# All gates of a hybrid S5 / mLSTM block by a seven-product block scheme, in two phases

## The chip, the cores and the metric

The kernel runs on one core of one Trainium2 chip. The metric is the device time of one execution in microseconds (us). The core has a tensor engine (PE, with its weight loads shown as PEld), VectorE (DVE), ScalarE (ACT), GpSimd (POOL) and SyncE (SP). SP issues nearly all transfers, POOL a few; all data that doesn't fit on chip passes through DRAM.

## The reference

One decoder block for 1024 tokens, with 16 learned meta tokens ahead (LEN = 1040), and D_MODEL = 1024. What matters here:

```python
p = h @ w_in + b_in          # columns [u_s5 | q | k | v | o | i | f | g_s5 | g_m]
y_s5 = GLU(GELU(S5(u_s5)))   # z[:, :1024] * sigmoid(z[:, 1024:]), z = gelu(..) @ w_glu
hm   = HeadNorm(mLSTM(silu(conv(q, k)), v, i, f))          # 4 heads of 256
y_m  = (sigmoid(o) * hm) @ m_w_out
mix  = sigmoid(g_s5) * y_s5 + sigmoid(g_m) * y_m
h    = LN(alpha * h + mix @ w_o)
h    = LN(alpha * h + relu(h @ w_up + b_up)**2 @ w_down)
```

o, g_s5 and g_m are the three gates: each is a projection of h with 1024 columns, that is eight tiles of 128 features, followed by a sigmoid. All of it is float32.

## The kernel before

*Products.* Every float32 operand is split into a high part, rounded to the fast matmul format, and the remainder: hi on ScalarE (a copy), lo = x - hi on VectorE. A product is then three matmuls, hi*hi, hi*lo and lo*hi (`mm3`, L229; the matmuls themselves are L240 to L242). The normalised input, transposed, lies on chip as `hT_hi` and `hT_lo`.

*Jobs.* The first half of the kernel is a list of jobs in the order of the string `ORDER`: q (with k), v, u, o, g (g_s5), then eight GLU jobs, the g_m jobs and eight jobs of the output projection of the mLSTM (`ym_job`). A job has one or two weight tiles of 128 x 1024. They are fetched one or two jobs ahead by SP and split (`split_w`: whi L220, wlo L221) while the job before runs (`job.after`). The functions of o and g_s5 jobs are `o_job` and `gs_job`: 128 features, eight blocks of 128 inputs, two halves of 512 tokens, three matmuls each, so 48 matmuls. An o job multiplies its sigmoid onto the finished head, `HM`, at once (L921), so the main loop forces the mLSTM lane forward until the head is there (`HMREADY`).

*Lanes.* Beside the jobs there are generators for the work off PE's main stream: the convolution, the mLSTM (`mlstm`), S5 (`s5_batch`, four batches), the token sums (`t_prep`), the scaled residual (`ah_scale`) and an early part of the feed-forward weights (`up_early`). `pump` moves them forward as matmuls are issued, at paces given in `PACE`. A planner with a model of the engines then puts every instruction into its engine's queue. The queue of each engine is static and executed in order.

*Seven products.* The g_m gates are computed in pairs of feature tiles. The product of a 2 x 2 block matrix of weights (two feature tiles by two halves of the inputs) with a 2 x 2 block matrix of h (two halves of the inputs by two halves of the tokens) is made of seven block products rather than eight, with sums of weight blocks (`wsums`: n1, n2, on VectorE) and sums of token blocks (made once by `t_prep`, kept in `t_dr`). A block product is four blocks of 128 inputs by three matmuls, 12. Four pairs: the plain products come in two jobs (`gme_job`), the others in one long job (`gm_pairs`), which loads the sums over the room of `hT` (`t_hi`, `t_lo`, by POOL's queue). The feed-forward layers use the same scheme.

*After the jobs* come the projection w_o, a LayerNorm, and the two feed-forward layers, from about 800 us to the end. The change doesn't touch them.

Of the kernel before, what the change touches and what calls it, by code (L numbers as in the profile page):

```python
# [120 lines left out]
def decoder_block(  # L121
# [73 lines left out]
    class Job:  # L195
        def __init__(self, loads, run):
            self.loads, self.run = loads, run
            self.raw, self.w, self.tag, self.ran = None, None, None, set()

# [15 lines left out]
    def split_now(job, later=False):  # L215
        job.w = []
# [39 lines left out]
    e_dr = dram.tile([2, P, 512], F32, name="e_dr")  # L256
    sgm_dr = dram.tile([KT, P, SEQ], F32, name="sgm_dr")
# [52 lines left out]
    QK, VT, HM, HMREADY = {}, {}, {}, set()  # L310
# [152 lines left out]
    def mlstm(h):  # L463
# [67 lines left out]
        def N(half, hm):  # L531
# [7 lines left out]
            for f in range(2):  # L539
                if half == 0:  # L540
                    HM[2 * h + f] = slot("hmF")
                ps = sdps("pt")
                for i in range(4):
                    t_.transpose(ps[:, i * P:(i + 1) * P], hraw[:, i * DV + f * P:i * DV + (f + 1) * P], ident)
                a_.activation(HM[2 * h + f][:, half * 512:(half + 1) * 512], ps, AF.Copy,
                              scale=mngt[:, 2 * h + f:2 * h + f + 1])
                yield 1.2
# [13 lines left out]
        HMREADY.update((2 * h, 2 * h + 1))  # L561
# [352 lines left out]
    hm_dr = dram.tile([KT, P, D], F32, name="hm_dr")  # L914

    def o_job(f):
        def evac(bi, c0, c1, ps):
            if bi == 0:
                o_job.s = slot("osig")
            a_.activation(o_job.s[:, c0:c1], ps, AF.Sigmoid, bias=bft[:, JO + f:JO + f + 1])  # L920
            v_.tensor_tensor(HM[f][:, c0:c1], HM[f][:, c0:c1], o_job.s[:, c0:c1], op=OP.mult)  # L921

        def done():
            nc.sync.dma_start(hm_dr[f], HM.pop(f)[:, :D])
        fm_job(JO + f, HALF, META, evac, done)
# [19 lines left out]
    def gs_job(f):  # L945
        def evac(bi, c0, c1, ps):
            if bi == 0:
                SG[f] = slot("sgs")
            a_.activation(SG[f][:, c0:c1], ps, AF.Sigmoid, bias=bft[:, JGS + f:JGS + f + 1])
        fm_job(JGS + f, HALF, META, evac)  # L950

    def glu_job(f):
        def run(job):
            if f == 0:
                lanes["s5c"].drain()
                lanes["s5"].drain()
                lanes["s5g"].drain()
            (wh, wl), = job.w
# [61 lines left out]
    GT, GR, GW, GC, GE = {}, {}, {}, {}, {}  # L1020

    def gt_load(n, tiles):
        GT[n] = tiles
        for i in range(4):
            g_.dma_start(tiles[i], t_dr[n - 1, :, i // 2, 2 * (i % 2):2 * (i % 2) + 2, :].rearrange("p k s -> p (k s)"))

    def gme_job(*ps):
        def run(job):
            if ps[0] == 2:
                for p in range(4):  # L1030
                    gr_load(p)
                gt_load(2, [slot("gt", F32R)[:, 0:1024] for _ in range(4)])
            chain, e = {}, {}
            for q in range(2):
                for i, p in enumerate(ps):
                    wh, wl = job.w[i]
                    if q == 0:
                        chain[p] = mmps()
                        e[p] = slot("gme")
                    terms = [(wh[:, (4 * q + j) * P:(4 * q + j + 1) * P], wl[:, (4 * q + j) * P:(4 * q + j + 1) * P],  # L1040
                              bh, bl) for j, (bh, bl) in enumerate(hT_blk(q, 0))]
                    mm3(chain[p], terms, part=(q == 0, True), skip=q == 1)
                    if q == 0:
                        a_.activation(e[p][:, 0:512], chain[p], AF.Copy)
                        if i == 0:
                            job.after()
                    else:
                        a_.activation(e[p][:, 512:1024], chain[p], AF.Sigmoid, bias=bft[:, JGM + 2 * p:JGM + 2 * p + 1])
                        nc.sync.dma_start(sgm_dr[2 * p, :, 0:512], e[p][:, 512:1024])
                        if p < 2:  # L1050
                            nc.sync.dma_start(e_dr[p], e[p][:, 0:512])
                        else:
                            GE[p] = e[p]
                if ps[0] == 2:
                    for z in (2 * q, 2 * q + 1):
                        gr_sums(z)
                        gw_split(z, 3)
        all_jobs.append(Job([(wf[JGM + 2 * p].rearrange("p k f -> p (k f)"), 1024) for p in ps], run))

    def gr_load(p):  # L1060
        GR[p] = [slot("gmr"), slot("gmr")]
        for i in range(2):
            nc.sync.dma_start(GR[p][i][:, :D], wf[JGM + 2 * p + i].rearrange("p k f -> p (k f)"))
        if p < 2:
            GE[p] = slot("gme")
            nc.sync.dma_start(GE[p][:, 0:512], e_dr[p])

    def gr_sums(p):
        r0, r1 = GR[p]
        n1, n2 = wsums(r0[:, 0:512], r0[:, 512:1024], r1[:, 0:512], r1[:, 512:1024])  # L1070
        GR[p] = {3: n2[:, 0:512], 4: r1[:, 512:1024], 5: n1[:, 0:512], 6: n1[:, 512:1024], 7: r1[:, 0:512]}

    def gw_split(p, n):
        x = GR[p].pop(n)
        o = slot("gmw", F32R)
        a_.activation(o[:, 0:512], x, AF.Copy)
        v_.tensor_tensor(o[:, 512:1024], x, f32(o[:, 0:512]), op=OP.subtract)
        GW[p, n] = o
        if n == 4:
            GR.pop(p)  # L1080

    GSEQ = [(p, n) for n in (3, 6, 5, 7, 4) for p in range(4)]

    def g_step(p, n):
        w = GW.pop((p, n))
        e = GE[p]
        b1, b2 = (bft[:, JGM + 2 * p + i:JGM + 2 * p + i + 1] for i in range(2))
        if n in (3, 6):
            ps = mmps()
        elif n == 5:  # L1090
            ps = sdps()
        else:
            ps = GC[p, "b"]
        if n == 3:
            blk = hT_blk(1, 1)
        else:
            t = GT[{4: 4, 5: 1, 6: 2, 7: 3}[n]]
            blk = [(t[j // 2][:, (j % 2) * 512:(j % 2) * 512 + 512], t[2 + j // 2][:, (j % 2) * 512:(j % 2) * 512 + 512])
                   for j in range(4)]
        terms = [(w[:, j * P:(j + 1) * P], w[:, 512 + j * P:512 + (j + 1) * P], bh, bl)  # L1100
                 for j, (bh, bl) in enumerate(blk)]
# [906 lines left out]
```

## Time and profile before

| | |
|---|---|
| three runs | 1540.72, 1542.88 (median), 1544.22 us |
| profiled execution | span of 1538.6 us; the page gives no other time of it |
| sigmoids of the o and g_s5 jobs | 197 to 562 us |
| evacuation of the GLU jobs | 571 to 652 us |
| later products of the g_m pairs | 662 to 720 us |
| evacuation of the mLSTM's output projection | 725 to 814 us |
| ScalarE, POOL | 41% and 7% busy |

Busy time of PE is modelled, and a matmul's own duration (375 ns on average for 512 columns) overlaps with the next one's; their spacing is what counts. A busy share is an average over stages. A line such as L240 is that of a helper, so that rows are told apart by the tiles they write and read. Idle time of an engine that is not the bottleneck costs nothing.

### The profile page before, as it was taken

What the parts mean: (1) busy time and instruction counts of PE and PEld (TensorE: products, weight loads), DVE (VectorE), ACT (ScalarE), POOL (GpSimd) and SP (SyncE); (2) the same over time, 40 slices, a digit from 0 to 9 for tenths busy, and PEclk for the clock granted to TensorE, in tenths of its full rate; (3) what the DMA queues carried; (4) which work ended last, traced back from release to release, by engine and by line L of the source; (5) the groups of instructions that cost most, each with busy time, mean ns of one, the idle gap of its engine ahead of it and who ended that gap; (6) DMA issues with size and microseconds to landing.
All of it is one profiled execution on the core that took longest, in us unless ns stands there. A gap on an engine that the chain in (4) does not pass through costs nothing.

```text
span 1538.6 us, 20771 instructions
## 1 busy us (share of the span) xinstructions
PE 1514.8 (98%) x7652; PEld 1279.8 (83%) x7652; DVE 1061.5 (69%) x2062; ACT 625.8 (41%) x996; POOL 102.4 (7%) x180
## 2 busy tenths in 40 slices
PE   9999999999999999999999999999999999999997
PEld 9999978998888888878878887888888888888886
DVE  7567867668968758675348574766666689766786
ACT  6623455324264443234015243444444534433440
POOL 0000000432214000010000001000000000000000
PEclk9999999999999999999999999999999999999999
DMA  9402265522332689878243238544444897766642
GB/s 333 143 5 88 72 203 159 174 64 61 113 91 71 184 292 355 317 281 322 102 149 139 83 119 271 178 149 145 150 142 133 276 381 280 246 234 232 211 178 96
DMA packets 148597, 277.71 MB, mean 181 GB/s; under 512 B 18488, under 2 KB 69120, under 8 KB 148496
## 3 DMA queue, kind: packets, MB, share of 16 engines
q1 hardware_dynamic: 143168, 256.99, 49.7%
q0 software_dynamic: 5328, 19.40, 3.9%
q8 instruction: 60, 0.98, 0.3%
q14 instruction: 41, 0.34, 0.1%
HBM read 188.00 MB, written 87.17 MB: 179 GB/s over the span
## 4 chain that ended last, share of the span: by engine, by line
PE 64%; issue 27%; DVE 5%; DMA 2%; ACT 1%; POOL 0%; POOLq 0%; SPq 0%; DVEq 0%; ACTq 0%
PE mm L240 16%; PE mm L241 15%; PE mm L242 15%; PE sd L240 3%; PE sd L241 3%; PE sd L242 3%; PE mm L236 2%; PE mm L274 1%; PE pn L504 1%; PE pn L505 1%; PE pu L508 1%; PE warm L1262 1%; DMA wpre<-wu_dr 1%; DMA wiB<-wrow_dr 1%; DMA t_hi<-t_dr 1%
## 5 line engine op out<-in xcount | busy, mean ns | idle before, releaser
L240 PE MATMUL mm<-hT_hi,whi 128*128 128x512 f32 (+3 forms) x480 | 180.0, 375 | 0.0
L242 PE MATMUL mm<-hT_hi,wlo 128*128 128x512 f32 (+3 forms) x480 | 177.9, 373 | 0.1
L241 PE MATMUL mm<-hT_lo,whi 128*128 128x512 f32 (+3 forms) x480 | 177.7, 370 | 0.0
L241 PEld LDWEIGHTS mm<-hT_lo,whi 128*128 128x128 f32 x480 | 90.3, 188 | 13.4 <-issue 1.2
L242 PEld LDWEIGHTS mm<-hT_hi,wlo 128*128 128x128 f32 x480 | 90.3, 188 | 13.0 <-DVE wlo L221 0.3
L240 PEld LDWEIGHTS mm<-hT_hi,whi 128*128 128x128 f32 x480 | 90.3, 188 | 12.9 <-issue 0.7
L1703 ACT ACTIVATE dah<-da 128x1024 fp32r<-128x1024 f32 x56 | 58.6, 1052 | 88.8 <-PE sd L241 36.7
L241 PE MATMUL sd<-dwl,dah 128*128 128x512 f32 x240 | 94.3, 393 | 0.0
L240 PE MATMUL sd<-dwh,dah 128*128 128x512 f32 x240 | 94.1, 393 | 0.0
L242 PE MATMUL sd<-dwh,dal 128*128 128x512 f32 x240 | 93.9, 392 | 0.0
L1707 ACT ACTIVATE dwh<-wdr 128x1024 fp32r<-128x1024 f32 x56 | 58.9, 1054 | 79.1 <-DMA wdr<-in_wdn_dram 23.2
L221 DVE TENSOR_TENSOR wlo<-wraw,whi 128x1024 fp32r<-128x1024 f32 (+1 forms) x56 | 68.0, 1222 | 30.8 <-ACT whi L220 15.8
L240 PE MATMUL mm<-dwh,dah 128*128 128x512 f32 (+1 forms) x224 | 84.4, 377 | 0.0
L241 PE MATMUL mm<-dwl,dah 128*128 128x512 f32 (+1 forms) x224 | 84.4, 377 | 0.0
L242 PE MATMUL mm<-dwh,dal 128*128 128x512 f32 (+1 forms) x224 | 84.2, 377 | 0.0
L220 ACT ACTIVATE whi<-wraw 128x1024 fp32r<-128x1024 f32 (+1 forms) x56 | 58.4, 1055 | 61.9 <-PE mm L241 20.2
L1704 DVE TENSOR_TENSOR dal<-da,dah 128x1024 fp32r<-128x1024 f32 x56 | 68.1, 1218 | 20.7 <-ACT dah L1703 20.1
L1708 DVE TENSOR_TENSOR dwl<-wdr,dwh 128x1024 fp32r<-128x1024 f32 x56 | 68.1, 1218 | 11.7 <-ACT dwh L1707 11.2
L240 PE MATMUL mm<-whi,hT_hi 128*128 128x256 f32 (+1 forms) x256 | 73.5, 287 | 0.0
L241 PE MATMUL mm<-wlo,hT_hi 128*128 128x256 f32 (+1 forms) x256 | 73.0, 285 | 0.0
L242 PE MATMUL mm<-whi,hT_lo 128*128 128x256 f32 (+1 forms) x256 | 73.0, 285 | 0.0
L240 PE MATMUL mm<-th,wuh 128*128 128x512 f32 x156 | 61.7, 396 | 0.0
(490 smaller groups left out, 3885.2 us busy)
## 6 DMA issues: line engine op xcount, KB each, us to landing
da<-act_dr SPq DMA_DIRECT2D x56, 512.0 KB, 5.1
wdr<-in_wdn_dram SPq DMA_DIRECT2D x56, 512.0 KB, 6.2
wraw<-in_wf_dram SPq DMA_DIRECT2D x32, 512.0 KB, 4.7
wur<-in_wup_dram SPq DMA_DIRECT2D x32, 512.0 KB, 4.3
act_dr<-upy SPq DMA_DIRECT2D x64, 256.0 KB, 2.7
wu_dr<-wpre SPq DMA_DIRECT2D x21, 512.0 KB, 6.5
wpre<-wu_dr POOLq DMA_DIRECT2D x21, 512.0 KB, 5.3
t_dr<-tpo SPq DMA_DIRECT2D x16, 512.0 KB, 5.9
```

Source lines behind the costliest of these rows:

```text
L220: a_.activation(hi[:, :n], r[:, :n], AF.Copy)
L221: todo.append(lambda e=v_, r=r, hi=hi, lo=lo, n=n: e.tensor_tensor(lo[:, :n], r[:, :n], f32(hi[:, :n]), op=OP.subtract))
L236: t_.matmul(ps, tm[i], tm[j], start=(w == 0 and k == 0), stop=(w == 2 and k == n - 1))
L240: t_.matmul(ps, ah, bh, start=(i == 0 and part[0]), stop=False, skip_group_check=skip)
L241: t_.matmul(ps, ah, bl, start=False, stop=False, skip_group_check=skip)
L242: t_.matmul(ps, al, bh, start=False, stop=(i == n - 1 and part[1]), skip_group_check=skip)
L274: t_.matmul(ps[:, :P], job.first[:, k * P:(k + 1) * P], HF[c0 // P][:, k * P:(k + 1) * P], start=(k == 0), stop=(k == KT - 1))
L504: t_.matmul(pn[:, :257], qi[:, c0:c0 + n], Cs[c][:, :257], start=True, stop=False)
L1703: a_.activation(ah[:, :D], a[:, :D], AF.Copy)
L1704: v_.tensor_tensor(alo[:, :D], a[:, :D], f32(ah[:, :D]), op=OP.subtract)
L1707: a_.activation(wh, raw[i], AF.Copy)
L1708: v_.tensor_tensor(wl, raw[i], f32(wh), op=OP.subtract)
```

## The change

All 24 gate tiles are now computed in 12 pairs by the seven-product scheme: p = 0 to 3 for o, 4 to 7 for g_s5, 8 to 11 for g_m. Each pair is worked in two phases.

Phase A (`ga_job`, a0 to a11 in `ORDER`) uses the plain token blocks: products 1, 2 and 3. It sums and splits the weights (`ga_prep`), stores the weight sums that phase B needs (`gw_dr`), the partial results (`e_dr`) and one finished quarter of the gate (`sig_dr`). Pairs 9 to 11 (`TAIL`) put off products 2 and 3 until the first three quarters of `hT` aren't needed any more, and the token sums are then loaded over the plain blocks, in place (`t_load`, four times, POOL's queue).

Phase B (`gb_job`, b0 to b7 ahead of the GLU jobs, b8 to b11 behind them) loads the weight sums and partial results again, splits them (`gb_prep`), and does products 6, 5, 7 and 4; product 4 of a pair runs within the next pair's job.

Finished gates are read back from DRAM: those of g_s5 by the GLU jobs (`sg_fetch`), those of g_m as before (`ms_fetch`), and those of o together with the heads (`hmo_load`), where the multiplication now is. A head goes to DRAM as soon as it is normalised, and no job waits for one. `up_early` and `ah_scale` start later, with the second and the first GLU job.

```diff
-ORDER = "q0 q1 v0 v1 q2 q3 o1 o0 o2 v2 o3 u0 u1 v3 u2 g0 u3 o4 o5 g1 o7 o6 g6 g2 g5 g3 g7 e0 g4"
+ORDER = "q0 q1 v0 v1 q2 q3 a0 a1 v2 a2 a3 u0 u1 v3 u2 a4 u3 a5 a6 a7 a8 a9 a10 a11 b0 b1 b2 b3 b4 b5 b6 b7"
+TAIL = (9, 10, 11)
+HMO_AT = 9
-LANE_AT = {"t_prep": "q3", "ah_scale": "g4", "up_early": "g7"}
+LANE_AT = {"t_prep": "q3", "ah_scale": "glu", "up_early": "glu2"}
...
     def split_now(job, later=False):
+        if job.prep:
+            job.w = job.prep(job.raw)
+            job.raw = None
+            return
...
     def hmo_load():
         rs = {}
         for k in range(KT + 2):
             if k < KT:
-                rs[k] = slot("hmr")
-                nc.sync.dma_start(rs[k][:, :D], hm_dr[k])
+                rs[k] = slot("hmr"), slot("ogr")
+                nc.sync.dma_start(rs[k][0][:, :D], hm_dr[k])
+                nc.sync.dma_start(rs[k][1][:, :D], sig_dr[k])
             if k >= 2:
-                HMO[k - 2] = split_act(rs.pop(k - 2), "hmo")
+                hm, og = rs.pop(k - 2)
+                v_.tensor_tensor(hm[:, :D], hm[:, :D], og[:, :D], op=OP.mult)
+                yield 0.6
+                HMO[k - 2] = split_act(hm, "hmo")
             yield 0.6
...
+    TB = {1: (0, 0), 2: (0, 1), 3: (1, 0), 4: (1, 1)}
+    def t_load(n):
+        kh, half = TB[n]
+        c = slice(META + 512 * half, META + 512 * half + 512)
+        for z, x in enumerate((hT_hi, hT_lo)):
+            g_.dma_start(x[:, 4 * kh:4 * kh + 4, c], t_dr[n - 1, :, z])
+    def gate_mm(ps, w, kh, half, start):
+        hi, lo = w
+        mm3(ps, [(hi[:, j * P:(j + 1) * P], lo[:, j * P:(j + 1) * P], bh, bl)
+                 for j, (bh, bl) in enumerate(hT_blk(kh, half))], part=(start, True), skip=not start)
...
+    def ga_prep(p):
+        def prep(raw):
+            r0, r1 = raw
+            n1, n2 = wsums(r0[:, 0:512], r0[:, 512:1024], r1[:, 0:512], r1[:, 512:1024])
+            nc.sync.dma_start(gw_dr[p, 0], n1[:, :D])
+            nc.sync.dma_start(gw_dr[p, 1], r1[:, :D])
+            hi, lo = split_act(r0, "gmw")
+            o = slot("gmo", F32R)
+            a_.activation(o[:, 0:512], n2[:, 0:512], AF.Copy)
+            v_.tensor_tensor(o[:, 512:1024], n2[:, 0:512], f32(o[:, 0:512]), op=OP.subtract)
...
+    def ga_step(p, n):
+        w, e, ps = GA[p]
+        if n == 1:
+            GA[p][2] = ps = mmps()
+            gate_mm(ps, w[1], 0, 0, True)
+            a_.activation(e[:, 0:512], ps, AF.Copy)
+        elif n == 2:
+            gate_mm(ps, w[2], 1, 0, False)
+            x = mid.tile([P, 512], F32, tag="gso", bufs=1, name="gso")
+            a_.activation(x, ps, AF.Sigmoid, bias=bft[:, gate_tile(p):gate_tile(p) + 1])
+            gate_out(p, 0, 0, x)
+        else:
+            px = mmps()
+            gate_mm(px, w[3], 1, 1, True)
+            v_.tensor_tensor(e[:, 512:1024], px, e[:, 0:512], op=OP.add)
+            nc.sync.dma_start(e_dr[p], e[:, :D])
+    def ga_job(p):
         def run(job):
+            GA[p] = [job.w, slot("gme"), None]
+            if p == TAIL[0]:
+                t_load(2)
+            ga_step(p, 1)
+            job.after()
+            if p not in TAIL:
+                ga_step(p, 3)
+                ga_step(p, 2)
+                GA.pop(p)
+            elif p == TAIL[-1]:
+                t_load(1)
+                for n, t in ((2, 3), (3, 4)):
+                    for q in TAIL:
+                        ga_step(q, n)
+                    t_load(t)
...
+    def gb_job(p):
+        def run(job):
+            if p == HMO_AT:
+                lanes["s5"].add(hmo_load())
+            last = list(GB)
+            GB[p] = dict(w=job.w, e=job.w.pop("e"))
+            gb_step(p, 6)
+            job.after()
+            gb_step(p, 5)
+            for q in last:
+                gb_step(q, 4)
+            gb_step(p, 7)
+            if p in (7, 11):
+                gb_flush()
...
-        if j.tag and j.tag[0] == "o":
-            while int(j.tag[1:]) not in HMREADY:
-                lanes["cv"].drain()
-                lanes["ml"].step()
```

More of the change, by code (lines that the diff above doesn't have):

```diff
@@ L1018, in quarter_sums @@
         v_.tensor_tensor(b21, b21, b22, op=OP.subtract)
[L1020 to L1027, printed above, removed]
-        def run(job):
[L1029 to L1071, printed above, removed]
@@ new lines, in ga_job @@
+    def ga_job(p):
+        def run(job):
+            GA[p] = [job.w, slot("gme"), None]
[13 more added lines that the diff above has]
+                    t_load(t)
+                GA.clear()
+        j = gate_tile(p)
+        all_jobs.append(Job([(wf[j + i].rearrange("p k f -> p (k f)"), 1024) for i in range(2)], run))
+        all_jobs[-1].prep = ga_prep(p)
@@ new lines, in gb_flush @@
+    def gb_flush():
+        for p in list(GB):
+            gb_step(p, 4)
+    def gb_job(p):
[12 more added lines that the diff above has]
+                gb_flush()
+            if p == 10:
@@ L1136, in gm_pairs @@
                 ms_fetch(0)
-                job.after()
-            if i == len(GSEQ) - 1:
+            if p == 11:
                 ms_fetch(1)
-            g_step(p, n)
-            if p == 3 and n == 3:
-                t_hi = h8.tile([P, KT, LEN], F32R, tag="hT_hi", name="t_hi")
-                t_lo = h8.tile([P, KT, LEN], F32R, tag="hT_lo", name="t_lo")
-                for j, m in enumerate((1, 3, 4)):
-                    gt_load(m, [x[:, 2 * j + z, 0:1024] for x in (t_hi, t_lo) for z in range(2)])
@@ L1146, in gm_pairs @@
-            if p == 3 and n == 6:
-                GT.pop(2)
-            if p == 3 and n == 5:
-                lanes["s5"].add(hmo_load())
+        all_jobs.append(Job([(gw_dr[p, i], 1024) for i in range(2)], run))
+        all_jobs[-1].prep = lambda raw: gb_prep(p, raw)
     def ms_fetch(f):
@@ L1428, in decoder_block @@
         j.w = None
+    for l in lanes.values():
+        l.drain()
     ring_ctx.close()
```

153 lines of the change are left out of this document (64 added, 89 removed).

## The prediction

> **What bounds the kernel now.** I read the page first, then the busy times by window, the waits of the tensor engine (PE), the chain of waits around the S5 scan, and the rows of single tiles.
>
> ```profile
> span 1538.6 us, 20771 instructions
> PE 1514.8 (98%) x7652; PEld 1279.8 (83%) x7652; DVE 1061.5 (69%) x2062; ACT 625.8 (41%) x996; POOL 102.4 (7%) x180
> ```
>
> ```profile
> 180.00:560.00 380.00, 373.05 (x2098) 323.50 (x2097) 274.34 (x763) 164.54 (x258) 75.79 (x114) 1.00 0.43 130
> 655.00:720.00 65.00, 63.08 (x272) 50.70 (x271) 44.93 (x65) 31.08 (x44) 6.34 (x12) 1.00 0.81 296
> 960.00:1190.00 230.00, 230.00 (x992) 186.13 (x991) 147.73 (x208) 105.34 (x153) 0.00 (x0) 1.00 0.45 148
> 230.00:240.00 10.00, 7.66 (x39) 5.95 (x38) 6.52 (x24) 6.87 (x11) 0.00 (x0) 0.83 0.00 0
> 220.00:230.00 10.00, 8.00 (x39) 5.99 (x39) 6.12 (x26) 3.47 (x9) 0.21 (x4) 1.00 0.34 106
> 340.00:420.00 80.00, 78.38 (x453) 69.40 (x452) 73.89 (x200) 26.34 (x50) 20.23 (x26) 1.00 0.32 92
> ```
>
> Columns: stretch, its length, busy time and count of PE, PEld, DVE (VectorE), ACT (ScalarE) and POOL, then clock, DMA share and GB/s. PE is the bound, with hardly a hole. Where it runs without one (960 to 1190, all 512 wide) a matmul takes 230 / 991 = 0.232 us. VectorE is 72% busy from 180 to 560, the stretch that the o and g_s5 jobs fill, and 92% from 340 to 420. It stays harmless there because an o or g_s5 job gives PE 48 matmuls (11.1 us) for one weight split and a little evacuation: PE always has products ready. The rows at 220 to 240 are the exception, the forced run of the mLSTM lane ahead of job o1: 2.0 + 2.3 us idle, and the clock at 0.83 for 10 us.
>
> ```profile
> PE pt L544 <- DVE hraw L537: 2.3, 1, 2.3
> PE sd L240 <- DMA t_hi<-t_dr: 1.9, 1, 1.9
> ```
>
> These are the two longest waits of PE in the whole span.
>
> **The change, part by part.** *Products.* Before, 16 plain jobs issue 16 x 48 = 768 gate matmuls, and the four g_m pairs 4 x 84 = 336. Now twelve pairs issue 12 x 84 = 1008. 96 fewer x 0.232 = **-22.3 us**, all on PE's path.
>
> *Waits that go.* No job waits for a head, so the hole at 220 to 240 goes: 2.0 + 2.3 + 10 x 0.17 = **-6.0**. The token-sum wait at its old place goes, 65.00 - 63.08 = **-1.9**; what is late next is the first sum of the new phase B (below). The 1.6 us idle in 340 to 420 is replaced by what I count next, **-1.6**.
>
> *VectorE.* A plain job cost it one 1024-wide split, and an o job two multiplications. A pair now costs four 512-wide sums, 3.5 splits of 1024 and six 512-wide additions, some 10.0 us for 19.5 us of PE. The gating multiplication (eight 1024-wide) moves into the stretch before the output projection.
>
> ```profile
> L921 DVE TENSOR_TENSOR hmF<-hmF,osig x16: 679/692/1700, 201.2 to 475.2; 128x512 f32<-128x512 f32 x16
> L1113 DVE TENSOR_TENSOR gmx<-mm,gme x4: 679/686/691, 668.8 to 674.4; 128x512 f32<-128x512 f32 x4
> L1319 DVE TENSOR_TENSOR wus<-gmr x4: 683/684/685, 652.1 to 665.5; 128x512 f32<-128x512 f32 x4
> L940 DVE TENSOR_TENSOR hmol<-hmr,hmoh x8: 1214/1224/1226, 686.7 to 710.0; 128x1024 fp32r<-128x1024 f32 x8
> L537 DVE TENSOR_SCALAR hraw<-hraw,hmv,hny x32: 396/407/414, 163.5 to 471.3; 128x256 f32<-128x256 f32 x32
> ```
>
> ```profile
> 342.81 1.38 DVE hraw L537 x4
> ```
>
> Four hraw take 1.38, not 4 x 0.407 = 1.63: instructions in a row overlap by 0.08. So I enter 0.60 for 512 wide and 1.14 for 1024 wide. The S5 batch's own rows in the chain:
>
> ```profile
> 360.08 0.61 DVE s5w L849
> 360.69 0.61 DVE s5w L850
> 361.30 0.67 DVE s5Ri L750
> 361.96 0.61 DVE s5Z L853
> 363.60 2.99 DVE s5w L859 x8
> 366.59 0.58 DVE s5Z L869
> 367.18 0.60 DVE s5w L872
> 368.98 0.60 DVE s5w L877
> 374.51 1.24 DVE wlo L221
> ```
>
> A whole batch needs 6 x 0.61 + 2.99 + 8 x 0.60 = 11.5 us of VectorE in a run, and in the kernel before PE works beside it on g0.
>
> VectorE executes in the order in which it was issued, so that order tells more than the mean load. In the issue order of the changed kernel I looked for pieces that begin with a VectorE instruction waiting for a PE result and end with one that PE waits for. VectorE's work in such a piece, less what PE has to do between the same two points, is a hole in PE.
>
> 1. From the denominators of the mLSTM chunk (dd) just before job u3 to the normalised head (hraw): a whole S5 batch stands between, 11.5, with s5Ri 0.67, C 0.4 and 16 short ones 2.5: 15.0 us. PE has 3 products of the mLSTM and 8 transposes, 2.2 us: job a4's second product stands behind the head's transposes. Hole **12.8**.
> 2. From a5's third product to a7's weights: a batch 11.5, five S5 products of 0.67, ten 512-wide sums, additions and splits 6.0, two 1024-wide splits 2.3, short ones 2.0: 25.1. PE: 52 gate matmuls 12.1 and small ones 6.2, together 18.3. Hole **6.8**.
> 3. From b8's last product to the first weights of the output projection: 8 gatings and 8 splits of the heads 18.2, eleven additions 6.6, b11's two splits 2.3, eight sums and splits for the feed-forward weights 4.8, the weight split 1.1: 33.0. PE: 91 matmuls, 21.1. Hole **11.9**.
> 4. Five small ones (2.5, 2.3, 2.0, 1.0, 0.3): **8.1**.
>
> Together **+39.6**. The same count on the order of the kernel before finds one hole, 1.7 us, and the wait row above has it at 2.3. That is why I trust it. It sees VectorE alone, so it is nearer a floor than a mean.
>
> *Clock.* The hole of 4.3 us at 220 to 240 cost 1.7 more by the clock. Holes 1 and 3 are longer; I take 1.7 for each, **+3.4** (ends: 0 if they fall into pieces, 6). The Trainium skill (TensorE: Matmul & The Clock Gate, Part 1) says that the array falls to half clock after an idle window of about 3.4 us and needs as long to come back; by that rule, as an estimate, each long hole costs 1.7 us more. Its window agrees with the 0.83 of the row.
>
> *Token sums.* Sum 1 can be fetched only when a11's first product has read the block it overwrites. Its first reader, b0's product 5, stands 10.9 us of PE later (38 gate matmuls, and 2.1 of the mLSTM and S5). The nearest rows:
>
> ```profile
> t_lo<-t_dr POOLq DMA_DIRECT2D x6, 512.0 KB, 6.7
> t_hi<-t_dr POOLq DMA_DIRECT2D x6, 512.0 KB, 14.4
> ```
>
> By t_lo it is hidden, by t_hi it is 3.5 late, by both in a row 10.2. I take **+3.5**: sums 3 and 4 and the reloaded weights are issued right behind it.
>
> *At no cost.* 104 more transfers, some 51 MB to and from DRAM (weights and sums of phase A, the stored gates): the DMA share of 0.43 between 180 and 560 covers them, and if it does not, that is rival B. ScalarE's additional splits lie under its 41%. SP's additional issues lie under PE's products; what is queued behind one that waits is the next weights, fetched one or two jobs ahead.
>
> *Sum*: -22.3 - 6.0 - 1.9 - 1.6 + 39.6 + 3.4 + 3.5 = **+14.7** on the span of 1538.6: 1553.3. The page gives the span alone; the median of the three runs is 4.3 above it, which I carry over: 1557.6, say **1558**.
>
> **Rivals.** *A, faster: the products win.* If the order in which VectorE's queue is issued isn't what PE waits for in holes 1 and 3, since the S5 and head work ahead is done before PE gets there, they go with their clock: 14.7 - 12.8 - 11.9 - 3.4 = -13.4, so 1529. It decides as soon as the holes together stay under 39.6 - 14.7 = 25 us. For it: at 340 to 420 VectorE was 92% busy and cost PE only 1.6. Against it: there PE had g0 and o4 to run, and in the new order the transposes of the head stand ahead of the gate's products.
>
> *B, slower still: transfers.* In the stretch b8 to b11 the order has 22 MB of transfers for 41.8 us of PE; the busiest row of the trace reaches:
>
> ```profile
> 680.00:700.00 20.00, 18.08 (x78) 14.37 (x77) 13.33 (x18) 7.66 (x10) 1.58 (x3) 1.00 1.09 405
> ```
>
> 22 MB at 405 GB/s take 54 us, 12 more than PE has; it runs beside hole 3 if all goes well. If it comes on top, and the fetches of phase A (two weights, two stores, one sum and a gate, 2.9 MB per 8.4 us of PE, 345 GB/s) are late as well by some 8 us, the time is 1558 + 20 = 1578. The Trainium skill (DMA: Bandwidth & Descriptors, Issuing engines are not separate DMA queues) says that transfers issued from different engines share the same 16 DMA engines; by that rule the sums on POOL's queue find no room of their own, which speaks for this rival. The 14.4 beside the 6.7 agrees.
>
> *C, no change.* Half of the holes are covered by reserve the count does not see: 14.7 - 15 = about 0, so 1543.
>
> **How the numbers follow.** Mine has 0.60, A 0.16, B 0.18, C 0.06. The range leaves out most of A and the far end of B: 1541 to 1580; mine alone is 1548 to 1567. 0.2% (3 us) is about what a measurement of this kernel can tell from no change. Faster 0.17 (A and a little of C), same 0.06, slower 0.77.
>
> **What would show it.** 96 fewer matmuls at about 0.232 us. No hole where the heads were forced. A hole of over 8 us in PE just before the products of u3, ended by hraw; PE waiting for gmwl about a6 and a7; and 8 to 15 us at the start of the output projection, ended by hmol or wlo, or by a DMA of ogr or wmo (B). The clock falls below 1.00 behind them. VectorE above 80% from the first gate job to the GLU, against 72%. If PE's idle time in that half of the kernel grows by less than 22 us, I am wrong, and A holds.

## The result and the profile after

The changed kernel takes 1606.4 us (median of four runs, 1603.7 to 1608.4) against 1542.8 us of the kernel before. The ratio is 1.042 with a 95% interval of 1.0402 to 1.0439: slower by 64 us, and above the range that was forecast (1541 to 1580). The profiled execution is the slowest of the four, one reason why the two spans below lie 68 us apart and not 64.

The head of the page, with the busy times, and the mean granted clock:

```profile
span 1606.7 us, 20950 instructions
PE 1521.0 (95%) x7556; PEld 1279.7 (80%) x7556; DVE 1123.2 (70%) x2142; ACT 636.8 (40%) x1008; POOL 98.3 (6%) x172
...
core 0: 1606.7 us, clock 0.977
```

```profile
core 0: 1538.6 us, clock 0.997
```

The second fence is the same view of the kernel before. The 68.1 us between the two spans fall apart without any model. PE's idle time is span less busy time: 1538.6 - 1514.8 = 23.8 before, 1606.7 - 1521.0 = 85.7 after, **+61.9**. PE's busy time grew by 6.2 although 96 matmuls (7652 to 7556, 22.3 us) are gone, so the others take **+28.5** longer. 61.9 + 28.5 - 22.3 = 68.1. The clock is enough to explain the 28.5: at 0.977 in place of 0.997, and with half speed as the only lower step seen here (last section), 2 x 0.023 x 1606.7 = 74 us of the span passed at half clock, against 9 us before. Half of the difference, 32 us, is what that costs if PE has work all the while.

Where it is, by window (columns as in the prediction), kernel after:

```profile
100.00:620.00 520.00, 458.32 (x2565) 400.57 (x2564) 392.43 (x1034) 208.94 (x328) 82.69 (x124) 0.95 0.59 191
620.00:820.00 200.00, 188.18 (x785) 150.72 (x784) 128.24 (x158) 65.91 (x86) 0.00 (x0) 0.97 0.87 321
820.00:1500.00 680.00, 679.78 (x2966) 551.62 (x2965) 455.35 (x670) 275.05 (x438) 11.21 (x21) 1.00 0.57 192
180.00:560.00 380.00, 323.87 (x1774) 278.83 (x1773) 283.32 (x736) 146.77 (x237) 80.31 (x122) 0.94 0.63 202
600.00:740.00 140.00, 140.00 (x621) 114.18 (x620) 94.88 (x120) 50.88 (x69) 0.00 (x0) 1.00 0.88 329
360.00:380.00 20.00, 4.84 (x24) 3.71 (x25) 17.52 (x42) 4.38 (x8) 4.76 (x5) 0.70 0.35 107
400.00:420.00 20.00, 14.90 (x62) 11.49 (x62) 16.91 (x32) 7.35 (x17) 10.25 (x7) 0.83 1.08 339
420.00:440.00 20.00, 13.19 (x66) 10.43 (x65) 19.80 (x41) 3.79 (x7) 2.55 (x5) 0.99 0.75 231
210.00:220.00 10.00, 6.80 (x53) 6.31 (x52) 7.45 (x18) 2.17 (x4) 2.39 (x1) 0.89 1.12 339
220.00:230.00 10.00, 10.00 (x64) 9.53 (x63) 9.75 (x19) 5.04 (x10) 0.29 (x5) 0.76 0.87 304
```

```profile
100.00:620.00 520.00, 511.05 (x2886) 447.45 (x2885) 382.35 (x1005) 218.66 (x337) 78.19 (x116) 1.00 0.46 145
620.00:820.00 200.00, 197.86 (x854) 159.86 (x853) 111.88 (x171) 66.60 (x122) 10.76 (x20) 1.00 0.64 234
```

The second fence is the kernel before. In the stretch of the gate, mLSTM and S5 work PE was idle for 9.0 us before and 61.7 after; from 620 to 820 for 2.1 and 11.8. From 820 on PE's idle time is the same. The stretch from 600 to 740 has no hole at all at a DMA share of 0.88, against 0.59 from 100 to 620: the bytes alone don't hold PE up. The longest waits of PE from 100 to 820:

```profile
PE pt L553 <- DVE hraw L546: 14.6, 3, 12.2
PE mm L247 <- ACT gmwh L941: 6.0, 4, 3.0
PE mm L249 <- DVE gmwl L942: 5.8, 4, 2.9
PE mm L247 <- DVE gmx L1127: 5.2, 2, 3.7
PE mm L247 <- ACT whi L227: 4.6, 1, 4.6
PE mm L247 <- ACT gme L1064: 3.9, 2, 2.2
PE s5y L899 <- DVE s5w L887: 3.8, 1, 3.8
PE pu L517 <- DVE sw L505: 3.8, 1, 3.8
PE pn L513 <- DVE s5Z L851: 3.1, 1, 3.1
```

One large hole (hraw, 12.2) and then a long list of short ones, spread over split weights (gmwh, gmwl), evacuations of partial products (gmx, gme) and steps of the mLSTM and S5 (pu, pn, s5y). Before, the longest was 2.3.

### The profile page after: what moved, and what is told of

Same layout as the page of the kernel before. It is cut to its first block, busy times and chain, and to the rows that moved or that the text cites. A ratio compares the mean times of both kernels' runs of the same rounds, so it can differ in the third digit from the quotient of the medians.

```text
span 1606.7 us, 20950 instructions
## 1 busy us (share of the span) xinstructions
PE 1521.0 (95%) x7556; PEld 1279.7 (80%) x7556; DVE 1123.2 (70%) x2142; ACT 636.8 (40%) x1008; POOL 98.3 (6%) x172
## 4 chain that ended last, share of the span: by engine, by line
PE 66%; issue 16%; DVE 9%; DMA 5%; SPq 2%; ACT 1%; POOL 0%; POOLq 0%; ACTq 0%; DVEq 0%
PE mm L249 17%; PE mm L247 17%; PE mm L248 17%; PE sd L247 2%; PE sd L248 2%; PE sd L249 2%; PE mm L243 2%; DMA wiB<-wrow_dr 1%; PE mm L282 1%; PE pn L513 1%; PE pu L517 1%; PE warm L1270 1%; PE pn L514 1%; DMA tpr<-h_dr 1%; SPq L799 1%
## 5 line engine op out<-in xcount | busy, mean ns | idle before, releaser
L247 PE MATMUL mm<-hT_hi,gmwh 128*128 128x512 f32 x288 | 121.3, 422 | 15.1 <-ACT gmwh L941 6.0
L249 PE MATMUL mm<-hT_hi,gmwl 128*128 128x512 f32 x288 | 116.5, 410 | 5.8 <-DVE gmwl L942 5.8
L248 PE MATMUL mm<-hT_lo,gmwh 128*128 128x512 f32 x288 | 118.1, 410 | 0.0
L247 PE MATMUL sd<-dwh,dah 128*128 128x512 f32 x240 | 94.4, 394 | 0.0
L1711 ACT ACTIVATE dwh<-wdr 128x1024 fp32r<-128x1024 f32 x56 | 58.9, 1054 | 78.1 <-DVE wdr L1693 21.6
L247 PEld LDWEIGHTS mm<-hT_hi,gmwh 128*128 128x128 f32 x288 | 57.0, 198 | 30.7 <-ACT gmwh L941 7.5
L249 PEld LDWEIGHTS mm<-hT_hi,gmwl 128*128 128x128 f32 x288 | 56.5, 196 | 21.1 <-DVE gmwl L942 7.7
L248 PEld LDWEIGHTS mm<-hT_lo,gmwh 128*128 128x128 f32 x288 | 57.0, 198 | 12.3
L247 PE MATMUL mm<-hT_hi,whi 128*128 128x256 f32 (+2 forms) x192 | 64.4, 336 | 0.0
L248 PE MATMUL mm<-hT_lo,whi 128*128 128x256 f32 (+2 forms) x192 | 63.8, 332 | 0.0
L249 PE MATMUL mm<-hT_hi,wlo 128*128 128x256 f32 (+2 forms) x192 | 63.4, 332 | 0.0
```

The costliest lines, as they stand in the source:

```text
L247: t_.matmul(ps, ah, bh, start=(i == 0 and part[0]), stop=False, skip_group_check=skip)
L248: t_.matmul(ps, ah, bl, start=False, stop=False, skip_group_check=skip)
L249: t_.matmul(ps, al, bh, start=False, stop=(i == n - 1 and part[1]), skip_group_check=skip)
L1711: a_.activation(wh, raw[i], AF.Copy)
```

## The experiments

All ratios below are to the kernel before; 0.1% is 1.5 us. "Against the changed kernel" is the difference of the ratio to 1.042, times 1541 us. A planner writes the order of every queue anew for each edit, and what another order alone is worth was not measured; so I read nothing into less than about 5 us of a single run.

| run | ratio (95%) | against the changed kernel | PE idle, us |
|---|---|---|---|
| changed kernel | 1.0420 (1.0402 to 1.0439) | | 85.7 |
| no_sums | 1.0410 (1.0395 to 1.0426) | -2 | 80.1 |
| no_sums_fewer | 1.0396 (1.0381 to 1.0412) | -4 | 84.4 |
| pool_stores | 1.0399 (1.0382 to 1.0416) | -3 | 80.6 |
| raw_again | 1.0418 (1.0403 to 1.0434) | 0 | 78.1 |
| no_gating | 1.0351 (1.0326 to 1.0376) | -11 | 70.7 |
| heads_forced | 1.0366 (1.0341 to 1.0390) | -8 | 71.1 |
| ml_pace | 1.0460 (1.0441 to 1.0479) | +6 | 82.9 |
| prep_early | 1.0380 (1.0364 to 1.0396) | -6 | 80.7 |
| a29 | 1.0644 (1.0626 to 1.0661) | +35 | 108.6 |
| fresh_bank | 1.0489 (1.0471 to 1.0508) | +11 | 94.4 |
| no_split | 1.0205 (1.0188 to 1.0222) | -33 | 60.6 |
| no_evac | 1.0187 (1.0169 to 1.0204) | -36 | 58.2 |
| no_both | 1.0033 (1.0022 to 1.0044) | -60 | 46.2 |
| no_both_forced | 0.9917 (0.9890 to 0.9944) | -78 | 30.2 |
| all_real | 1.0318 (1.0297 to 1.0339) | -16 | 67.4 |
| plain_forced | 1.0034 (1.0021 to 1.0047) | | 28.9 |
| plain_free | 1.0081 (1.0063 to 1.0099) | | 33.9 |
| b28 | 1.0135 (1.0118 to 1.0152) | | 36.0 |

### One load at a time: sums, stores, bytes, gating

The first theories: V, VectorE's order and load, as in the prediction; S, SP's queue, where stores that wait hold back the weights issued behind them (the prediction had put SP's issues at nothing); D, the additional bytes.

```diff
# no_sums
-            n1, n2 = wsums(r0[:, 0:512], r0[:, 512:1024], r1[:, 0:512], r1[:, 512:1024])
+            slot("wus"), slot("wus")
+            n1, n2 = r0, r1
# pool_stores: the stores to gw_dr, e_dr and sig_dr
-            nc.sync.dma_start(gw_dr[p, 0], n1[:, :D])
+            g_.dma_start(gw_dr[p, 0], n1[:, :D])
# raw_again
-            nc.sync.dma_start(gw_dr[p, 0], n1[:, :D])
-            nc.sync.dma_start(gw_dr[p, 1], r1[:, :D])
...
-        all_jobs.append(Job([(gw_dr[p, i], 1024) for i in range(2)], run))
+        all_jobs.append(Job([(wf[gate_tile(p) + i].rearrange("p k f -> p (k f)"), 1024) for i in range(2)], run))
# no_gating
-                v_.tensor_tensor(hm[:, :D], hm[:, :D], og[:, :D], op=OP.mult)
```

> Phase A takes the raw weights where it should take their sums (four VectorE sums per pair left out, 48 in all; transfers, stores and buffers as in the changed kernel). Theory V (VectorE's order sets PE's holes): 48 x 0.60 = 29 us less VectorE, hole 2 and most of the small holes go, 8 to 15 us faster than the 1606.4 of the changed kernel, 1591 to 1598. Theory S (the stores hold SP's queue and the weights behind them come late): the stores no longer wait for the sums (48.7 us of waiting on that queue), 10 to 25 us faster, 1581 to 1596. Theory D (too many bytes): no change, 1606.

> All stores of the gate phases (weights and sums, partial results, gates) are issued on POOL's queue in place of SP's; same bytes, same VectorE work. Theory V: no change, 1602 to 1610. Theory S: what waits behind stores on SP's queue (weights, S5 copies) comes in time, 20 to 35 us faster, 1571 to 1586. Theory D: no change, 1606.

> The weights and sums of phase A are not stored (24 stores of 512 KB, 12.6 MB, left out); phase B loads the raw weights again in their place, so that its products 4 to 7 use other weights. Theory V: no change, 1602 to 1610. Theory S: half of the stores that wait on SP's queue are gone, 10 to 20 us faster, 1586 to 1596. Theory D: 12.6 of 329 MB less, at 300 to 400 GB/s some 30 to 40 us of transfer time, of which at most a third on the path: 1594 to 1606, spread over the whole of phase A.

> The multiplication of the heads by the stored output gates is left out (8 VectorE instructions of 1.2 us; the gates are still loaded). Theory V: hole 3 ahead of the output projection shrinks by 8 x 1.14 = 9 us and the clock holds there, 9 to 12 us faster, 1594 to 1597. Theories S and D (the read-back is late by its transfers): no change, 1606.

Measured: 2, 3, 0 and 11 us faster. S and D fall as single causes: with all the stores on another queue, and with 24 transfers (12.6 MB) fewer, PE's idle time is 5 and 8 us shorter, and the time gains 3 and nothing. V falls in its plain form too: 48 sums, 32 us of VectorE's busy time (1123.2 to 1091.2), are worth nothing that can be told. Only the gating came out as V had it. The waits of PE from 730 to 800 in the kernel without it:

```profile
PE mm L247 <- ACT whi L227: 2.0, 1, 2.0
PE mm L247 <- DVE gme L1119: 1.4, 2, 0.8
PE mm L247 <- ACT gmwh L940: 0.7, 1, 0.7
PE mm L249 <- DVE gmwl L941: 0.3, 1, 0.3
PE mm L247 <- DVE gmx L1126: 0.2, 1, 0.2
```

4.6 us in place of 11.8 (the changed kernel's waits on whi, gmx, gmwh and gmwl there: 4.6 + 3.7 + 3.0 + 0.5), and the granted clock of that window rose from 0.90 to 0.98.

### The force on the mLSTM

The prediction booked the forced heads as a hole that goes. But the last normalised head (the last time in each row) is 91 us later in the changed kernel, among the S5 batches:

```profile
L546 DVE TENSOR_SCALAR hraw<-hraw,hmv,hny x32: 379/409/415, 166.2 to 562.5; 128x256 f32<-128x256 f32 x32
```

The prediction's row of the kernel before ends at 471.3. Theory H: without the force the mLSTM's chain falls on the S5 batches. It was tried on both kernels: heads_forced puts the force back into the changed one, plain_forced and plain_free are the kernel before with stored gates and heads gated at the read-back, with and without the force.

```diff
# heads_forced
+HEAD_BY = {"a0": 0, "v2": 1, "a5": 2, "a9": 3}
...
+        while j.tag in HEAD_BY and HEAD_BY[j.tag] not in READY:
+            lanes["cv"].drain()
+            lanes["ml"].step()
# ml_pace
-PACE = {"ml": 0.56, ...
+PACE = {"ml": 0.42, ...
# plain_forced, from the kernel before
             a_.activation(o_job.s[:, c0:c1], ps, AF.Sigmoid, bias=bft[:, JO + f:JO + f + 1])
-            v_.tensor_tensor(HM[f][:, c0:c1], HM[f][:, c0:c1], o_job.s[:, c0:c1], op=OP.mult)
...
-            nc.sync.dma_start(hm_dr[f], HM.pop(f)[:, :D])
+            nc.sync.dma_start(sig_dr[f], o_job.s[:, :D])
# plain_free, from plain_forced
-        if j.tag and j.tag[0] == "o":
-            while int(j.tag[1:]) not in HMREADY:
-                lanes["cv"].drain()
-                lanes["ml"].step()
```

> The changed kernel with the mLSTM lane forced ahead again, at the places in PE's work where the kernel before did so: head 0 must be issued before a0, head 1 before v2, head 2 before a5, head 3 before a9. Theory H (no job waits for a head any more, so the mLSTM runs on to 562 in place of 471 and its serial chain falls on the S5 batches): the last normalised head comes back to about 480, the waits at 340 to 580 shrink, 20 to 35 us faster in spite of the forced holes, 1571 to 1586. Theory V (VectorE's order and load in the pairs): the forced hole of the kernel before comes on top, 1606 to 1613.

> One number of the changed kernel: the pace of the mLSTM lane 0.42 in place of 0.56, so that its steps are issued against a quarter less PE time. Theory H: the last normalised head comes at about 480 to 500 and the time falls by 10 to 25 us, 1581 to 1596. Theory V: the same work in another order, 1602 to 1611.

> The kernel before with one part of the change alone: the output gates are stored and the heads gated when they are read back; plain products, and the mLSTM lane forced as before. Theory H: nothing of it stands in the mLSTM's way, 1540 to 1546. Theory V: 9 us more VectorE ahead of the output projection, which has 288 matmuls there (67 us) to hide it: 1540 to 1550.

> The same, and no head is forced: the part of the change named last, without the seven products. Theory H: the mLSTM lane lags and falls on the S5 batches, 15 to 40 us slower than with the force, 1557 to 1585. Theory V: the forced hole is gone, 6 us faster than with it, 1534 to 1542.

The force is worth 8 us in the changed kernel and 1.0081 - 1.0034 = 7 us in the plain one: the direction of H, and less than half of what it forecast (20 to 35 and 15 to 40). Storing the gates and gating at the read-back costs the plain kernel 5 us. The reason that H gave doesn't hold as it stands:

```profile
L547 DVE TENSOR_SCALAR hraw<-hraw,hmv,hny x32: 401/407/1269, 163.7 to 493.5; 128x256 f32<-128x256 f32 x32
```

```profile
L546 DVE TENSOR_SCALAR hraw<-hraw,hmv,hny x32: 399/405/1252, 160.3 to 488.2; 128x256 f32<-128x256 f32 x32
```

First heads_forced, then ml_pace. They bring the last head forward by 69 and 74 us, and the one is 8 us faster, the other 6 slower. So the place of the last head isn't what counts by itself; why the force helps where a quicker pace does not stays open.

### Buffers and lead

Theory R: a pair takes eight of the 30 shared buffers where a plain job takes three, and what PE waits for waits itself for a buffer. In the timeline of the changed kernel the split that PE stands for begins 2.40 us late, when a copy of the S5 lane has landed, which shares nothing with it but, it seems, a buffer; ScalarE stands 6.81 us in the same way:

```profile
476.90 0.39 PE L248 MATMUL mm<-hT_lo,gmwh 128*128 128x512 f32 x1
...
478.87 1.22 DVE L942 TENSOR_TENSOR gmwl<-wraw,gmwh 128x1024 fp32r<-128x1024 f32 x1 [2.40 <-DMA s5Mx<-s5Kt]
...
480.15 0.50 PE L249 MATMUL mm<-hT_hi,gmwl 128*128 128x512 f32 x1 [2.86 <-DVE gmwl L942]
...
481.95 0.63 ACT L1054 ACTIVATE gmo<-wus 128x512 fp32r<-128x512 f32 x1 [6.81 <-DMA e_dr<-gme]
```

Theory W: the preparation is issued with too short a lead. R was tried by taking buffers away.

```diff
# a29 (b28: the same line of the kernel before, with 28)
-    big = ctx.enter_context(tc.tile_pool(name="big", bufs=30, side="left"))
+    big = ctx.enter_context(tc.tile_pool(name="big", bufs=29, side="left"))
# no_sums_fewer, from no_sums
-            slot("wus"), slot("wus")
# prep_early
+            job.after()
             ga_step(p, 1)
-            job.after()
...
+            job.after()
             gb_step(p, 6)
-            job.after()
```

> The changed kernel with 29 buffers of 4224 bytes in the shared pool in place of 30. Theory R (a pair takes eight buffers, raw, sums, splits and partial results, where a plain job takes three, and what PE waits for waits itself for a buffer that a late store or copy still reads): one buffer fewer costs 5 to 15 us, 1611 to 1621. Theory W (weights and partial results are prepared too short ahead, whatever the buffers): 1603 to 1609.

> The kernel before with 28 buffers in place of 30. Theory R: plain jobs have buffers to spare, two fewer cost 0 to 5 us, 1541 to 1546. Should it cost as much per buffer as in the changed kernel, the buffers are no property of the pairs.

> As the run without weight sums (raw weights in place of the sums, 48 VectorE instructions left out), and now the two buffers of the sums aren't taken either: six buffers per pair in phase A in place of eight. Theory R: 5 to 15 us faster than the 1603.7 with the buffers, 1589 to 1599. Theory W: as with the buffers, 1601 to 1606.

> The changed kernel with each pair's weights summed and split one product earlier: issued ahead of the first product of the pair before, not behind it, 12 matmuls (2.8 us) more of lead. Theory W: the waits of PE for split weights (19.5 us between 100 and 820) fall by half and their clock with them, 8 to 15 us faster, 1591 to 1598. Theory R: earlier work holds its buffers longer, no gain or a loss, 1604 to 1615.

a29 is 35 us slower, which looks like a proof of R and is none: look at where.

```profile
100.00:620.00 520.00, 452.58 (x2528) 395.18 (x2527) 386.89 (x1031) 207.48 (x324) 83.00 (x124) 0.93 0.58 189
620.00:820.00 200.00, 187.19 (x777) 149.65 (x776) 127.48 (x157) 67.38 (x88) 0.00 (x0) 0.96 0.86 319
820.00:1500.00 680.00, 664.69 (x2884) 534.53 (x2883) 439.67 (x656) 266.66 (x427) 11.20 (x21) 1.00 0.53 182
```

Up to 820 PE is idle for 67.4 + 12.8 = 80.2 us, 6.7 more than with 30 buffers; 15 us of idle time lie behind 820, in the layers that the change doesn't touch. The kernel before loses 21 us with two buffers fewer. Two buffers per pair less in no_sums_fewer give 2 us against no_sums; that is a weak test, since nothing writes or reads the two in no_sums, and how long they were held isn't shown. So buffers are scarce in the whole kernel, but what the pairs lose by them isn't shown to be more than some us; a test with more buffers was not made. W has 6 us of its 8 to 15, hardly more than I read anything into.

### Preparation and evacuation left out

What had not been taken away yet is the pairs' own work on VectorE and ScalarE. It has two parts: P, the weights (sums and splits); E, the evacuations between the seven products (copy and additions, with the partial result stored and loaded).

```diff
# no_split, in ga_prep: the split weights of the first pair are kept for all
+            if not KEPT:
                 hi, lo = split_act(r0, "gmw")
...
+            return KEPT
# in gb_prep
-        (h1, l1), (h2, l2) = split_act(n1, "gmw"), split_act(r1, "gmw")
+        return {"e": e, 5: KEPT[1], 6: KEPT[2], 7: KEPT[3], 4: KEPT[1]}
# no_evac, in ga_step and gb_step
-            a_.activation(e[:, 0:512], ps, AF.Copy)
-            v_.tensor_tensor(e[:, 512:1024], px, e[:, 0:512], op=OP.add)
-            nc.sync.dma_start(e_dr[p], e[:, :D])
...
-            v_.tensor_tensor(x12, ps, x12, op=OP.add)
-            v_.tensor_tensor(c["x"], ps, p1, op=OP.add)
...
-            a_.activation(x, x, AF.Sigmoid, bias=bias)
+            a_.activation(x, ps, AF.Sigmoid, bias=bias)
# all_real: prep_early, heads_forced and
-LANE_AT = {"t_prep": "q3", "ah_scale": "glu", "up_early": "glu2"}
+LANE_AT = {"t_prep": "q3", "ah_scale": "b7", "up_early": "glu"}
```

> Leaves out the preparation of the gate weights on VectorE and ScalarE: the three split weights of the first pair are used for all pairs and all products; the raw weights are loaded and stored as before, products and evacuations are as in the changed kernel. Theory P (PE stands behind weights that are split late, and VectorE and ScalarE behind those splits): the 19.5 us of waits for split weights go, and half of the mLSTM's 34 with most of the clock, 35 to 55 us faster, 1551 to 1571. Theory E (the seven partial products, each read by VectorE or ScalarE before the next may follow, bind PE): 5 to 15 us faster, 1591 to 1601.

> Leaves out the additions between the seven products (one ScalarE copy and six VectorE additions per pair) and the store and load of the partial results; each gate is the sigmoid of what its accumulator holds. Weights as in the changed kernel. Theory E: 35 to 55 us faster, 1551 to 1571. Theory P: the 9.1 us of waits for evacuations go and some of the mLSTM's, 10 to 18 us faster, 1588 to 1596.

> Both left out. Theories P and E each: little more than the larger of the two alone. Theory Q (VectorE and ScalarE work in order, so that either work delays the other and the mLSTM, and each covers for the other when it alone is taken away): 60 to 75 us faster, near the products' saving on the kernel with stored gates, 1530 to 1545, and the two alone give less than half of that.

> The changed kernel with three repairs that leave the result as it is: weights prepared one product earlier, the mLSTM forced ahead as in the kernel before, and the two lanes for the last layers started before the GLU (the residual's scaling at b7, the feed-forward weights at the first GLU job). If the gains add: 8 + 8.5 and 3 to 8 us from the stretch ahead of the output projection, 1582 to 1588. If they overlap: 1592 to 1598.

33, 36 and 60 us. Neither P nor E alone: each is about right on its own part (35 to 55 forecast) and too low on the other's, and the parts nearly add (33 + 36 = 69 against 60). Q has the size of the two together (60 to 75 forecast), but its reason, by which each would cover for the other, is refuted: each alone gives more than half of what they give together. They give more than the waits that they remove by name. The longest waits of PE, 100 to 820, without the preparation and without the evacuations:

```profile
PE pt L553 <- DVE hraw L546: 10.9, 2, 9.1
PE mm L247 <- DVE gmx L1128: 9.1, 1, 9.1
PE pS L503 <- ACT hmF L554: 8.4, 1, 8.4
PE s5y L898 <- DVE sw L505: 3.5, 1, 3.5
```

```profile
PE pt L553 <- DVE hraw L546: 9.9, 3, 8.9
PE s5z L843 <- DVE C L520: 4.5, 1, 4.5
PE mm L249 <- DVE gmwl L942: 4.1, 3, 2.3
PE mm L247 <- ACT gmo L1054: 3.2, 2, 2.3
PE pn L513 <- DVE C L522: 3.0, 1, 3.0
```

Summed over such rows, the waits for split weights fall from 19.5 to 2.5 us in no_split, and those for evacuations from 9.1 to nothing in no_evac; the mLSTM's fall as well, from 33.8 to 24.1 and 17.9. Its steps stand in the same queues. One rival to the queues isn't separated by these two runs: they free buffers too. In phase A, no_split takes five of a pair's eight no more (but keeps three throughout), and no_evac one, with its store and load. So it is shown that leaving this work out gains 60 us; how much of that goes by the queues and how much by the buffers is not. The three repairs of all_real give 16 us, where the sum of prep_early's and heads_forced's gains is 14: they add, and are far from enough.

### The accumulator, and the account closed

Two things were open. One way in which an evacuation could bind PE is theory K: products 2, 7 and 4 go on in an accumulator that another engine has to read first. And if preparation, evacuation and the missing force are all that stands between the products and their gain, then with all three out of the way the 22 us must appear.

```diff
# fresh_bank
-            gate_mm(ps, w[2], 1, 0, False)
+            ps = mmps()
+            gate_mm(ps, w[2], 1, 0, True)
...
-        ps = c["b"] if n in (4, 7) else mmps()
+        ps = mmps()
# no_both_forced: no_both with the force of heads_forced
```

> Products 2, 7 and 4 start in an accumulator of their own in place of adding to the one that ScalarE or VectorE has to read first; all copies, additions, splits and transfers stay, and the sums lack a term. Theory K (PE waits at the accumulator for the read between two products): the 9.1 us of waits for evacuations go with their clock, 10 to 20 us faster, 1586 to 1596. Theory Q (the additions cost by their place and time on VectorE and ScalarE): no change, 1601 to 1611.

> Preparation and evacuation of the gates left out as before, and the mLSTM forced ahead as in the kernel before. If the force is worth here the 7 to 8 us that it was worth twice: 1535 to 1540. The plain kernel with stored gates and the force had 1545.5, and the products are worth 22 us: if nothing else stands in their way, 1523 to 1530. Above 1540, the force and the rest overlap.

fresh_bank is 11 us slower. The waits for evacuations are gone (0.7 us are left), but those for split weights have grown from 19.5 to 41:

```profile
PE mm L247 <- ACT gmwh L941: 30.4, 4, 15.7
PE pt L553 <- DVE hraw L546: 15.3, 6, 11.9
```

K has nothing for it: those waits of PE went, and others stand in their place, since the work that ends them is still queued. The test isn't a clean one, because each pair now takes accumulators of its own from the shared five. It is also a warning against adding up the rows of waits as gains.

no_both_forced comes to 1526.3 us, 0.9917 of the kernel before, and by the ratios 18 us under plain_forced (1.0034), which has the same stored gates, read-back and force but plain products:

```profile
span 1523.6 us, 20533 instructions
PE 1493.4 (98%) x7556; PEld 1262.4 (83%) x7556; DVE 1004.0 (66%) x1976; ACT 588.9 (39%) x951; POOL 93.0 (6%) x172
```

PE is 98% busy again, and its busy time is 21.4 us under that of the kernel before (1514.8): the 22 us of the products. So the account closes to within 4 us: the saving is real, and preparation and evacuation (60 us) and the missing force (18 us here, 7 to 8 in the other two pairs of runs) take it back more than three times over. Of the kernels that leave nothing out, none is faster than the kernel before.

## Why the prediction was wrong, step by step

*Right.* The sign, and the steps that hold most of its named numbers. 96 matmuls fewer. Hole 1, the S5 batch ahead of hraw: 12.8 forecast, 12.2 measured, ended by hraw. Hole 2, from a5's third product (its matmuls end at 416) to a7's weights (first used at 443): 6.8 forecast, 6.81 measured, all of it in the row 420 to 440, with VectorE busy for 19.8 of the 20 us. But PE waits there for steps of the mLSTM and S5 within the piece (3.8 for s5w, 1.8 for sw), not for gmwl. Hole 3, the piece ahead of the output projection: 11.9 forecast, 11.8 measured (4.6 + 3.7 + 3.0 + 0.5), with VectorE all but packed from 747 to 779, and no_gating shows that it was mostly VectorE's work. It isn't one hole "at the start of the output projection": it came in three places, and only the 4.6 stand there, ended by ScalarE's whi, which had to follow a head that VectorE was still gating. So the count has the loss of a long piece to within a microsecond three times; that it is that close must be partly luck, since the kinds of wait were not as named. The bytes at no cost: held as far as it was tested, by raw_again (12.6 of the 51 MB) and by 140 us without a hole at a DMA share of 0.88. SP's issues at no cost: held within 3 us by pool_stores, against my own first suspicion. The token sums: hidden, as in the lower end; no wait on them among PE's.

*The sum, term by term.* Besides the -22.3 of the products, the +14.7 holds +35.3 of idle time and +1.7 of clock. The two spans differ by +61.9 of idle time and +28.5 of longer matmuls. Of the 53 us that the prediction missed, one half (26.6) is idle time and the other (26.8) is the clock; these are the two steps that failed.

*"Five small ones, 8.1": this step failed first.* PE's idle time from 100 to 820 grew from 11.1 to 73.5, by 62.4. Holes 1 to 3 make 30.8. The other 31.6, and 7.8 for the idle time that the prediction let go, 39 in all, stand against 8.1; 5.1 of them lie in the row 400 to 420 alone, ahead of hole 2. The search counted pieces of the order in which VectorE alone has too much to do. What no_split and no_evac show in its place is that the small instructions between a PE result and PE's next operand cost almost anywhere, 33 and 36 us: copy, addition and split pass through VectorE and ScalarE in turn, and the mLSTM's own short steps stand in the same queues. That it is the order of these queues, and not the buffers that the work holds, fits the rows of waits but isn't shown. The prediction called its count "nearer a floor than a mean" and then entered it as the mean.

*"Clock +3.4": mis-sized, and as costly.* Matmuls took 28.5 us longer, against +1.7 in the sum (3.4 less the 1.7 that was to go with the old hole). Only the two long holes were given a clock price. Between 100 and 820, 68 us passed at half clock in 13 stretches, of which 27 lie at holes 1 and 3; the rest came behind short holes (last section).

*"VectorE above 80%": wrong, and it would have led astray.* It was 283.32 / 380 = 75%, hardly more than before. no_sums takes 32 us off it for nothing, no_evac 46 us (1123.2 to 1077.6) for 36: what VectorE does counts more than how busy it is.

*"The hole at 220 to 240 goes, -6.0": wrong twice.* A hole of that price is still there, a little earlier: from 215 to 219 PE waits 1.7 us for mlo and 1.5 for hraw, and the clock falls. By the rows 210 to 220 and 220 to 230 that is 3.2 us idle and 10 x (0.11 + 0.24) = 3.5 by the clock, 6.7 us when counted as the prediction did. (Both holes lie beside job v2; the prediction's "ahead of job o1" misreads the row.) And the force that the prediction took for the cause was worth 7 to 8 us elsewhere. I asked what the wait cost and not what it kept in order.

*The rivals.* A's condition (the holes under 25 us together) failed at once: idle grew by 62. B named 1578 for transfers that are late; the time passed it, but no wait of PE on a transfer is among its rows of waits. The range ended where B ended because no case had the small waits in it.

## What to carry to other kernels

A scheme that trades matmuls for sums must be charged for its joints, not only for its arithmetic: here 96 matmuls (22 us) were bought with some 60 us of preparation and evacuation, though VectorE was no more than three quarters busy over the stretch. Count how often PE needs something that has passed through another engine since PE's last result, and treat a count of large holes as a floor. Before removing a forced wait, ask what it keeps apart; and when a resource is taken away as a test, see in which stretch the time was lost before believing it.

## What the runs showed of the hardware

PE fell to half clock behind shorter holes than I had reckoned with, and not by their length alone. Kernel after, by window:

```profile
132.54:135.95 3.41, 0.85 (x7) 0.51 (x5) 3.38 (x13) 0.79 (x4) 2.06 (x2) 1.00 0.78 317
135.95:139.37 3.42, 3.42 (x13) 3.42 (x12) 3.21 (x26) 0.71 (x2) 0.00 (x0) 0.50 0.02 7
535.31:538.72 3.41, 1.67 (x8) 0.89 (x6) 3.41 (x6) 0.00 (x0) 1.20 (x2) 1.00 0.00 0
538.72:542.14 3.42, 2.34 (x11) 2.06 (x12) 3.42 (x7) 1.08 (x2) 0.54 (x1) 1.00 0.17 18
569.44:572.86 3.42, 1.66 (x8) 0.94 (x7) 3.20 (x11) 1.59 (x2) 0.00 (x0) 1.00 0.56 173
572.86:576.27 3.41, 2.96 (x7) 2.39 (x8) 3.35 (x7) 1.62 (x4) 0.00 (x0) 0.50 0.97 296
```

Behind a hole of 2.6 us (up to 135.6) the clock is 0.50, and matmuls of 400 columns start 0.33 us apart, against 0.18 ahead of it. Behind one of 2.0 us (up to 573.3) it is 0.50 as well; behind one of 2.8 us (up to 539.8) it stays at 1.00. The rows are cut so that the clock's steps fall on their edges, and those edges form a grid: with the stretch from 100 to 825 cut every 3.413 us through 135.95, each of the 211 windows has a clock of 1.00 or of 0.50, and none lies between. heads_forced and fresh_bank fit a grid of the same step.

What decides, as far as these traces show, is how busy PE was in the window before. In the three traces a window at full clock in which PE was busy for 0.43 of the time or less was always followed by one at half clock, and one with 0.52 or more never; between them both happened (0.49 ahead of 538.72 and ahead of 572.86). So a hole of two or three us costs 3.4 us at half clock, 1.7 us of work, if it falls into one window, or shares it with other short ones, and may cost nothing if it lies across two.

The Trainium skill (TensorE: Matmul & The Clock Gate, Part 1) puts the drop behind an idle window of about 3.4 us; the length agrees with the 3.413 here, but the window need not be idle: PE busy for 0.40 of it sufficed. Waits of two or three us, which a kernel with spare work hides, aren't harmless once they come in a row.
